# Residual scaled at its reload, score products from split halves, and half-array products side by side, in a two-layer attention and expert kernel

## The chip, the cores and the metric

The kernel runs as one program on one core of a Trainium2 chip. The metric is the device time of one execution in microseconds (us), as the median of several runs. The core's engines are named as in the profile: PE (TensorE, matrix products; PEld is its weight load), DVE (VectorE), ACT (ScalarE), POOL (GpSimd), SP (SyncE, which issues all the DMAs here).

## The reference

256 tokens of width 1024 go through two layers. Each layer is attention, a residual LayerNorm, an expert mixer (PEER) and another residual LayerNorm. Cut to what matters here:

```python
# layer 0: differential attention, 8 heads of two 64-wide maps
q, k = rope(x @ Wq), rope(x @ Wk); v = x @ Wv
s = einsum('bhmqd,bhmkd->bhmqk', q, k) * 64**-0.5        # m = 0, 1
p = softmax(where(chunk_mask, s, -inf))
o = (p[:, :, 0] - lam * p[:, :, 1]) @ v                  # RMS norm per head, then @ w_o
# layer 1: stick-breaking attention, 16 heads of 64
z = einsum('bhqd,bhkd->bhqk', q, k) * 64**-0.5
tail = reverse_cumsum(log_sigmoid(-z)) - log_sigmoid(-z)  # strictly causal
o = exp(log_sigmoid(z) + tail) @ v                       # then @ w_o
# after each sub-layer f
x = layer_norm(ALPHA * x + f(x)) * g + b
# peer(x): scores of 8 heads x 2 x 128 keys, top 16, softmax gates of 128 experts a token;
#          out = (gates * gelu(x @ u.T)) @ v, with u, v of 16384 x 1024
```

All inputs and the output are float32. The result has to agree with the float32 reference.

## The kernel before, in words

Almost all the products are of one kind. A weight row block (128x1024, 512 KB) is loaded as `raw`, ACT rounds it to `h` (L145), DVE or POOL computes the rest `l = raw - h` (L150), and PE multiplies in three passes: h by the high part of the activations (xh), l by xh, h by their low part (xl). h, l, xh and xl are float32r, a form that PE multiplies in one pass; a product of two plain float32 operands stands in the trace as two instructions that each take longer. `raw`, `h` and `l` have three buffers each. In `stationary` (L235) the weights are PE's stationary operand and the output comes transposed, in `moving_steps` (L214) the activations are.

The program in order: the Q, K and V products of layer 0 with the first attention (up to 142 us of the span), a LayerNorm, `peer` of layer 0 (routing, 128 blocks of u, then 128 blocks of v, up to 951 us), a LayerNorm, the stick-breaking attention (966 to 1097 us), a LayerNorm, `peer` of layer 1, the last LayerNorm.

**First attention.** `tr` (L396) transposes Q and K on PE, ACT copies the result to plain float32 QT and KT. `s1(i)` (L451) makes the scores of heads 2i and 2i+1 for the token blocks b=1 and b=0: for each map m and head a product with 64 rows (half of PE's 128 rows; m says which half), followed at once by a mask product over all 128 rows (L463). DVE takes the maxima (L464), ACT the exponentials (L467), DVE combines the maps (L476); `s2` transposes the result (L487), `s3` multiplies by V (L498, L500). The products of V (L440) are put between them.

**Stick-breaking attention.** `s1(h)` (L581) makes one head's scores: two products with 64 rows (L585, L586) and two mask products over 128 rows (L588, L589). ACT computes exp and ln, `s2` adds the tail by products with a triangle (L598 to L600), `s3(c)` multiplies heads 2c and 2c+1 by V, with 64 output columns each (L609, L610).

**LayerNorm.** DVE adds the residual (L273) and takes the statistics (L276), POOL the power -0.5 (L297). Token block 0 is scaled on ACT (L305), block 1 on DVE in five pieces (L324); PE transposes (L314), ACT and DVE make the next xh and xl (L330 to L332) with gain and offset applied there. The next stage's first four weight blocks were loaded ahead (`prefetch`); the first three are split in halves called `ahead`: ACT makes h, POOL l (L174), of block 0 before the LayerNorm and of blocks 1 and 2 after the second power (`hold`). After that POOL also applies gain and offset to the natural-order copy `y` (`natural`, L338, L339), which is the next residual. In `peer`, y then goes to DRAM (`xres`) and comes back near the end of `peer` for the next LayerNorm.

What sets the order: the program is written as a stream for each engine, and a scheduler with a timeline of its own places the instructions of an engine where their operands and buffers come free; inside `manual_schedule` the written order holds. The accumulator banks of tag "w" are four; scores, transposes and results of both attentions share them.

Of the kernel before, what the change touches and what calls it, by code (L numbers as in the profile page):

```python
# [10 lines left out]
F32 = mybir.dt.float32  # L11
# [9 lines left out]
P = 128  # L21
# [37 lines left out]
def trunk(ctx: ExitStack, tc: tile.TileContext, x, xT, ln_g, ln_b, w_qkv, w_o_a, lam_p, subln, w_kv,  # L59
# [60 lines left out]
    class Units:  # L120
        def __init__(self):
            self.n = 0
            self.hold = None
# [32 lines left out]
        def prefetch(self, src, raws):  # L156
            self.raws = [reg(o, D) for o in raws]
            self.pre = []
            for d, raw in enumerate(self.raws):
                self.later(raw, src(d))  # L160
            for d in range(AHEAD):
                h = [work.tile([P, 512], F32R, name="ahead", tag="hw", bufs=RING) for _ in range(2)]
                for f in range(2):
                    queue_after(nc.scalar.activation(h[f], self.raws[d][:, f * 512:(f + 1) * 512], AF.Copy), self.h)  # L164
                self.pre.append([h])
                if d == 0:
                    self.low(d)

        def low(self, d, after=None):
# [3 lines left out]
            for f in range(2):  # L173
                o = nc.gpsimd.tensor_tensor(l[f], self.raws[d][:, f * 512:(f + 1) * 512], h[f].bitcast(F32), OP.subtract)  # L174
# [6 lines left out]
        def prefetched(self):  # L181
            for d in range(1, AHEAD):
                self.low(d, self.hold)
# [73 lines left out]
    def load_gb(layer, s):  # L257
        g, bb = reg(O_G, D), reg(O_G + D, D)
# [48 lines left out]
    def layer_norm(acc, res, y, layer, s, gb, xh, xl):  # L307
# [8 lines left out]
        with tc.manual_schedule(engines={mybir.EngineType.DVE, mybir.EngineType.Activation}):  # L316
# [3 lines left out]
            units.hold = rs.second()  # L320
            mv = rs.mv[1]
            for d0, d1 in ((0, 1), (1, 2), (2, 4), (4, 6), (6, 8)):
# [13 lines left out]
        def natural():  # L336
            for b in range(NB):
                queue_after(nc.gpsimd.tensor_tensor(y[:, b, :], y[:, b, :], gb[0], OP.mult), units.hold)  # L338
                nc.gpsimd.tensor_tensor(y[:, b, :], y[:, b, :], gb[1], OP.add)  # L339

        units.natural = natural
# [35 lines left out]
    def diff_attention(xh, xl):  # L377
# [3 lines left out]
        QT, KT = reg(8192, DC, T), reg(10240, DC, T)  # L381
# [14 lines left out]
        def tr(srcv, dstT, tag):  # L396
            for b in range(NB):
                for g in range(2):
                    pt = psum.tile([P, 4, P], F32, name=tag, tag=tag)
                    for c in range(4):  # L400
                        n = 4 * g + c
                        nc.tensor.transpose(pt[:, c, :], srcv[:, b, n * P:(n + 1) * P], ident)
                    nc.scalar.activation(dstT[:, 4 * g:4 * g + 4, b * P:(b + 1) * P], pt, AF.Copy)
# [47 lines left out]
        def s1(i):  # L451
            hs = slice(2 * i, 2 * i + 2)
            for b in (1, 0):
                nk = P * (b + 1)
                p = pview(i, b)
                for m in range(2):
                    ps = psum.tile([P, 2, nk], F32, name="w", tag="w")
                    ms = slice(m * 64, (m + 1) * 64)
                    for j in range(2):
                        o = ps[:, j, :]  # L460
                        h = 2 * i + j
                        nc.tensor.matmul(o, QT[ms, h, b * P:(b + 1) * P], KT[ms, h, 0:nk], start=True, stop=False)  # L462
                        nc.tensor.matmul(o[:, nk - 64:nk], identb, bmask, start=False, stop=True)  # L463
# [83 lines left out]
        gb = load_gb(0, 0)  # L547
# [14 lines left out]
        return acc, gb  # L562


    def stick_breaking(xh, xl):
# [5 lines left out]
        units.natural()  # L571
# [9 lines left out]
        def s1(h):  # L581
            c, r = h // 2, slice((h % 2) * 64, (h % 2) * 64 + 64)
            z = psum.tile([P, 512], F32, name="w", tag="w")
            zt[h] = z
            nc.tensor.matmul(z[:, 0:256], KT[r, c, 0:P], QT[r, c, :], start=True, stop=False, skip_group_check=True)  # L585
            nc.tensor.matmul(z[:, 256:384], KT[r, c, P:T], QT[r, c, P:T], start=False, stop=False,  # L586
                             skip_group_check=True)
# [15 lines left out]
        def s3(c, oh, ol):  # L603
            o = psum.tile([P, T], F32, name="w", tag="w")
            for k in range(2):
                h, r = 2 * c + k, slice(k * 64, k * 64 + 64)
                a = ab[h]
                hs = slice(h * 64, h * 64 + 64)
                nc.tensor.matmul(o[r, :], V[:, 0, hs], a[:, 0:256], start=True, stop=False, skip_group_check=True)  # L609
                nc.tensor.matmul(o[r, P:T], V[:, 1, hs], a[:, 256:384], start=False, stop=True,  # L610
                                 skip_group_check=True)
# [3 lines left out]
        for i in range(HB + 2):  # L615
            if i < HB:
                s1(i)
            if i >= 2:
                s2(i - 2)
# [6 lines left out]
        gb = load_gb(1, 0)  # L626
# [9 lines left out]
        return acc, gb  # L636


    def peer(layer, xh, xl, spill, o_res):
# [4 lines left out]
        units.natural()  # L644
# [315 lines left out]
        for s in range(n + 1):  # L960
# [56 lines left out]
    for layer in range(2):  # L1017
        acc, gb = diff_attention(xh, xl) if layer == 0 else stick_breaking(xh, xl)
        xh, xl = xtiles()
        yv = reg(y, NB, D)  # L1020
        layer_norm(acc, reg(res, NB, D), yv, layer, 0, gb, xh, xl)
# [3 lines left out]
        if layer == 0:  # L1025
            xh, xl = xtiles()
            layer_norm(acc, reg(res, NB, D), yv, layer, 1, gb, xh, xl)
# [47 lines left out]
```

## Time and profile before

| | |
|---|---|
| runs | 1926.5 us median of 3 (1920.65 to 1926.59) |
| profiled execution | 1923.61 us, its span 1921.8 us, mean granted clock 0.982 |
| busy | PE 1853.7, DVE 1241.8, ACT 914.5, POOL 212.6 us |
| first attention, from the first score to the last | 70.1 to 109.3 us |
| three inner LayerNorms: first residual add to the dense products of the next stage | 137.6 to 153.0, 951.2 to 966.6, 1093.0 to 1108.4 us |

A busy PE is not PE at its peak: a product's end is modelled, and products that wait in a row count as busy. So the start-to-start distances in the chain of waits are what a product costs.

### The profile page before, as it was taken

To read this page: it belongs to the slowest core of one execution; us is meant where nothing else is said; L and a number is where in the kernel's file an instruction comes from. 1 tells how busy PE (TensorE), PEld (TensorE's weight loads), DVE (VectorE), ACT (ScalarE), POOL (GpSimd) and SP (SyncE) were. 2 spreads that over 40 slices of the span, in tenths; PEclk is the share of its full clock that TensorE was granted. 3 is DMA by queue.
4 is the path that set the end of the run, shared out by engine and by line. 5 is a ranking of instruction groups with operands and counts; after the bars stand their busy time and mean duration, and the time that the engine had idled before them with its cause. 6 is when DMAs were issued, how large, how long until landed. Compare 5 with 4: busy or idle time off the path is not lost.

```text
span 1921.8 us, 30897 instructions
## 1 busy us (share of the span) xinstructions
PE 1853.7 (96%) x12248; PEld 1665.9 (87%) x12248; DVE 1241.8 (65%) x2379; ACT 914.5 (48%) x1244; POOL 212.6 (11%) x208
## 2 busy tenths in 40 slices
PE   8999989999999999999999999899999999999997
PEld 7778989898899999988798699899989999999886
DVE  5467978997555555565552479789965555555655
ACT  4444444555444444454447454455544444444543
POOL 5425400000000000000142253000000000000001
PEclk9888999999999999999999999999999999999999
DMA  6433544335565555575533235443355555555653
GB/s 217 172 124 110 178 141 154 121 111 197 181 205 185 187 187 196 177 245 192 208 130 133 110 131 177 143 145 113 130 197 187 179 188 193 186 187 188 241 196 131
DMA packets 90449, 325.40 MB, mean 169 GB/s; under 512 B 10176, under 2 KB 10560, under 8 KB 89664
## 3 DMA queue, kind: packets, MB, share of 16 engines
q1 hardware_dynamic: 90304, 323.43, 49.3%
q8 instruction: 96, 1.57, 0.3%
q14 instruction: 49, 0.40, 0.1%
HBM read 320.24 MB, written 3.15 MB: 168 GB/s over the span
## 4 chain that ended last, share of the span: by engine, by line
PE 80%; DVE 16%; issue 2%; DMA 1%; ACT 1%; POOL 0%; SPq 0%; ACTq 0%; POOLq 0%
PE acc L201 40%; PE w L808 28%; PE acc L246 4%; DVE l L150 3%; DVE gl L892 2%; DVE big L865 2%; DVE gh L892 2%; PE acc L440 1%; DVE oa L896 1%; PE w L246 1%; DVE big L324 1%; PE w L201 1%; PE w L462 1%; DVE big L699 1%; DVE big L701 1%
## 5 line engine op out<-in xcount | busy, mean ns | idle before, releaser
L145 ACT ACTIVATE h<-raw 128x1024 fp32r<-128x1024 f32 x579 | 607.5, 1060 | 853.2 <-PE acc L201 474.5
L150 DVE TENSOR_TENSOR l<-raw,h 128x1024 fp32r<-128x1024 f32 x526 | 645.0, 1238 | 533.8 <-ACT h L145 533.6
L808 PE MATMUL w<-xh,l 128*128 128x256 f32 x2048 | 579.6, 284 | 16.5 <-DVE l L150 16.5
L808 PE MATMUL w<-xh,h 128*128 128x256 f32 x2048 | 585.7, 286 | 2.1 <-ACT h L145 2.1
L808 PE MATMUL w<-xl,h 128*128 128x256 f32 x2048 | 580.0, 283 | 0.0
L808 PEld LDWEIGHTS w<-xh,l 128*128 128x128 f32 x2048 | 392.5, 192 | 22.4 <-DVE l L150 17.4
L808 PEld LDWEIGHTS w<-xh,h 128*128 128x128 f32 x2048 | 393.5, 192 | 7.9 <-ACT h L145 2.5
L201 PE MATMUL acc<-h,wl 128*128 128x512 f32 x1024 | 399.1, 391 | 0.0
L201 PE MATMUL acc<-l,wh 128*128 128x512 f32 x1024 | 398.7, 390 | 0.0
L808 PEld LDWEIGHTS w<-xl,h 128*128 128x128 f32 x2048 | 393.4, 192 | 4.8
L201 PE MATMUL acc<-h,wh 128*128 128x512 f32 x1024 | 278.1, 390 | 0.0
L201 PEld LDWEIGHTS acc<-h,wl 128*128 128x128 f32 x1024 | 192.8, 188 | 36.9
L201 PEld LDWEIGHTS acc<-l,wh 128*128 128x128 f32 x1024 | 192.5, 188 | 36.4
L201 PEld LDWEIGHTS acc<-h,wh 128*128 128x128 f32 x1024 | 188.1, 188 | 35.6
L150 POOL TENSOR_TENSOR l<-raw,h 128x1024 fp32r<-128x1024 f32 x53 | 128.2, 2421 | 169.7 <-ACT h L145 156.2
L174 POOL TENSOR_TENSOR ahead<-big,ahead 128x512 fp32r<-128x512 f32 x18 | 24.0, 1361 | 752.7 <-ACT ahead L164 752.7
L951 DVE TENSOR_TENSOR wl<-big,wh 128x512 fp32r<-128x512 f32 x128 | 87.0, 687 | 6.3 <-PE acc L201 5.7
L297 POOL TENSOR_TENSOR mv<-mv,mhalf 128x1 f32<-128x1 f32 x8 | 4.9, 609 | 752.0 <-DVE mv L296 752.0
L950 ACT ACTIVATE wh<-big 128x512 fp32r<-128x512 f32 x128 | 78.2, 620 | 9.2 <-PE acc L201 4.9
L907 PE MATMUL acc<-oa,gl 128*128 128x128 f16 x512 | 66.3, 220 | 14.5 <-DVE gl L892 13.0
L906 PE MATMUL acc<-oa,gh 128*128 128x128 f16 x512 | 70.4, 220 | 0.2 <-DVE gh L892 0.2
L866 ACT ACTIVATE big<-acc 128x344 f32<-128x344 f32 x128 | 51.5, 454 | 30.7 <-DVE big L865 30.7
(215 smaller groups left out, 1841.1 us busy)
## 6 DMA issues: line engine op xcount, KB each, us to landing
raw<-in_uT SPq DMA_DIRECT2D x256, 512.0 KB, 3.3
raw<-in_v SPq DMA_DIRECT2D x256, 512.0 KB, 3.3
raw<-in_w_qkv SPq DMA_DIRECT2D x23, 512.0 KB, 4.2
raw<-in_w_kv SPq DMA_DIRECT2D x12, 512.0 KB, 4.0
raw<-in_w_o_a SPq DMA_DIRECT2D x8, 512.0 KB, 4.0
big<-in_w_pq SPq DMA_DIRECT2D x8, 512.0 KB, 6.4
raw<-in_w_pq SPq DMA_DIRECT2D x8, 512.0 KB, 5.3
raw<-in_w_q SPq DMA_DIRECT2D x8, 512.0 KB, 4.3
```

The lines of the kernel that those rows point to most:

```text
L145: self.h = nc.scalar.activation(h, raw, AF.Copy)
L150: o = e.tensor_tensor(l, raw, h.bitcast(F32), OP.subtract)
L201: nc.tensor.matmul(acc[b][f], a[:, d, ts], w[:, fs], start=(first and q == 0), stop=(last and q == 2))
L246: nc.tensor.matmul(acc[n // 2][:, n % 2, :], w[:, c:c + P], a[:, d, :], start=(d == 0 and q == 0 and n % 2 == 0), stop=(d == DC - 1 and q ...
L808: nc.tensor.matmul(ps[:, k, :], w[:, ds], a[:, d, :], start=(d == 0 and q == 0), stop=(d == DC - 1 and q == 2))
L865: nc.vector.scalar_tensor_tensor(wv[:, 0:N_STORED], pv[:, 0:N_STORED], 1.0 / GS, wv[:, 0:N_STORED], OP.mult, OP.mult)
L866: nc.scalar.activation(wv[:, N_STORED:], pv[:, N_STORED:], AF.Copy, scale=1.0 / GS)
L892: nc.vector.tensor_tensor(dst.rearrange("p r (a b) t -> p r a b t", b=16), hi[:, rs].unsqueeze(3).to_broadcast([P, 4, 8, 16, 2]), lo[:, rs ...
L906: nc.tensor.matmul(ps[:, k, :], gh[:, m, :, e], oa[:, m, :, e], start=True, stop=False)
L907: nc.tensor.matmul(ps[:, k, :], oj[:, m, :, e], oa[:, m, :, e], start=False, stop=True)
L950: nc.scalar.activation(wh, s, AF.Copy)
L951: nc.vector.tensor_tensor(wl, s, wh.bitcast(F32), OP.subtract)
```

## The change

Four edits.

1. First attention: QT and KT are each kept as two float32r tiles, high (ACT) and low (DVE, new L407); a score is three products (high by high, high by low, low by high). For each token block and head the two maps, which lie on the two halves of PE's rows, are written next to each other, in two banks. One mask product serves both heads of a map.
2. Stick-breaking: `s1(c)` takes two heads, which lie on the two halves of PE's rows, and writes their products next to each other before the masks; `s3` writes the two heads' products next to each other.
3. LayerNorm: POOL makes l of `ahead` blocks 0 and 1 before the LayerNorm, DVE that of block 2 after xl[1]; the first block's passes come as h by xh, l by xh, h by xl; DVE scales token block 1 in four pieces, not five.
4. `natural` leaves POOL. In both `peer`s y goes to DRAM unscaled; near the end gain and offset are loaded once more (to a second place) and DVE scales the reloaded residual. In the stick-breaking attention DVE scales y right behind xl[7].

```diff
+                if d < AHEAD - 1:
+                    self.low(d, nc.gpsimd)
...
         def prefetched(self):
-            for d in range(1, AHEAD):
-                self.low(d, self.hold)
+            self.low(AHEAD - 1, nc.vector, self.xhl[1][1])
...
-                seq = [(n, q) for q in range(3) for n in range(8)]
+                seq = [(n, q) for q in (0, 2, 1) for n in range(8)]
...
-            for d0, d1 in ((0, 1), (1, 2), (2, 4), (4, 6), (6, 8)):
+            for d0, d1 in ((0, 2), (2, 4), (4, 6), (6, 8)):
...
+    def natural(y, gb, after=None):
+        for b in range(NB):
+            for c, op in enumerate((OP.mult, OP.add)):
+                o = nc.vector.tensor_tensor(y[:, b, :], y[:, b, :], gb[c], op)
...
+        QT = [quad("hw", RING), quad("hw", RING)]
+        KT = [quad("hw", RING), quad("oh", OH)]
...
+                h, l = (t[i] for t in dstT)
+                nc.scalar.activation(h, pt, AF.Copy)
+                nc.vector.tensor_tensor(l, pt, h.bitcast(F32), OP.subtract)
...
-                        nc.tensor.matmul(o, QT[ms, h, b * P:(b + 1) * P], KT[ms, h, 0:nk], start=True, stop=False)
-                        nc.tensor.matmul(o[:, nk - 64:nk], identb, bmask, start=False, stop=True)
+                for j in range(2):
+                    for q, (x, y) in enumerate(((0, 0), (0, 1), (1, 0))):
+                        for m in range(2):
+                            ms = slice(m * 64, (m + 1) * 64)
+                            nc.tensor.matmul(pss[m][:, j, :], QT[x][i][ms, j, b * P:(b + 1) * P], KT[y][i][ms, j, 0:nk],
+                                             start=(j == 0 and q == 0), stop=False, skip_group_check=True)
+                for m, ps in enumerate(pss):
+                    nc.tensor.matmul(ps[:, :, nk - 64:nk], identb, bmask.unsqueeze(1).to_broadcast([P, 2, 64]),
+                                     start=False, stop=True, skip_group_check=True)
...
-        gb = load_gb(0, 0)
...
+        natural(yv, gb, units.xhl[1][DC - 1])
...
+            for z, r in zip(zs, rows):
+                nc.tensor.matmul(z[:, 0:256], KT[r, c, 0:P], QT[r, c, :], start=True, stop=False, skip_group_check=True)
+            for z, r in zip(zs, rows):
+                nc.tensor.matmul(z[:, 256:384], KT[r, c, P:T], QT[r, c, P:T], start=False, stop=False,
+                                 skip_group_check=True)
...
+            for kb, (q0, c0, c1) in enumerate(((0, 0, 256), (P, 256, 384))):
+                for k in range(2):
...
-        gb = load_gb(1, 0)
...
                 pre["gb"] = load_gb(layer, 1)
                 nc.sync.dma_start(reg(o_res, NB, D), xres)
+                natural(reg(o_res, NB, D), load_gb(layer, 0, O_G - 4096))
```

PE, first attention, scores of the first two heads for b=1, before (L462 the score, L463 its mask; w_604 and w_612 are the banks of maps 0 and 1):

```order
L462 MATMUL w_604<-big_70 128x256
L463 LDWEIGHTS identb_74
L463 MATMUL w_604<-bmask_82,identb_74 128x64
L462 MATMUL w_604<-big_70 128x256
L463 LDWEIGHTS identb_74
L463 MATMUL w_604<-bmask_82,identb_74 128x64
L462 MATMUL w_612<-big_70 128x256
```

and now (L465 the score, L468 the mask, qk the split QT and KT; w_628 and w_629 the banks of the two maps), the first six of its twelve products, and then the scores of heads 4 and 5 for b=1 (w_789, w_790):

```order
L465 MATMUL w_628<-qk_106,qk_98 128x256
L465 MATMUL w_629<-qk_106,qk_98 128x256
L465 MATMUL w_628<-qk_110,qk_98 128x256
L465 MATMUL w_629<-qk_110,qk_98 128x256
L465 MATMUL w_628<-qk_106,qk_102 128x256
L465 MATMUL w_629<-qk_106,qk_102 128x256
...
L465 MATMUL w_789<-qk_112,qk_100 128x256
L465 MATMUL w_789<-qk_108,qk_104 128x256
L468 LDWEIGHTS identb_74
L468 MATMUL w_789<-bmask_82,identb_74 128x2x64
L465 MATMUL w_790<-qk_108,qk_100 128x256
```

Of the eight blocks of twelve scores (four pairs of heads, two token blocks) two alternate between the maps as written, three have the maps one after the other without a mask between, and in three the scheduler has put one map's mask before the other map's scores.

PE, stick-breaking attention, now: the first pair of heads (L590, L592 the scores, L599, L600 the masks), and a later head, followed by an earlier head's tail products (L609 to L611):

```order
L590 MATMUL w<-big 128x256 x2
L592 MATMUL w<-big 128x128 x2
L599 LDWEIGHTS identb
...
L590 MATMUL w<-big 128x256
L592 MATMUL w<-big 128x128
...
L600 MATMUL w<-cmask,identb 128x128
L609 MATMUL w<-big,ntri 128x256
L610 MATMUL w<-big,ntri 128x128
L611 MATMUL w<-big,none_78 128x128
```

Three of the eight pairs stand next to each other as written; in five the scheduler puts one head's masks before the other's scores, as before.

DVE, near the end of layer 0's `peer`, now (L149 the weight split, L959 the split of the weighted gates, L337 the four new operations on the residual):

```order
L149 TENSOR_TENSOR l_8687<-raw_8684,h_8686 128x1024
L149 TENSOR_TENSOR l_8705<-raw_8702,h_8704 128x1024
L337 TENSOR_TENSOR big_70<-big_70 128x1024 x2
L959 TENSOR_TENSOR wl_8890<-big_70,wh_8889 128x512
L337 TENSOR_TENSOR big_70<-big_70 128x1024 x2
L149 TENSOR_TENSOR l_8736<-raw_8733,h_8735 128x1024
```

They stand in front of two weight splits; before, nothing stood there but the L959 row. On SP the four loads of gain and offset now stand together in front of the same v block's load, where two stood; their earlier places (in front of the first w_o load of each attention) are empty, and the store to `xres` has moved to before the stage's last `w_pq` load.

## Rows read from the trace of the kernel before

**Rows 1.** The profile's page: busy us of each engine, share of the span, instructions.
```profile
PE 1853.7 (96%) x12248; PEld 1665.9 (87%) x12248; DVE 1241.8 (65%) x2379; ACT 914.5 (48%) x1244; POOL 212.6 (11%) x208
```
**Rows 2.** Waits of PE: who waited for whom, us in total, times, longest.
```profile
PE w L314 <- DVE big L324: 15.0, 15, 2.4
```
**Rows 3.** Chain of waits, 60 to 180 us, by line (shares of 120 us).
```profile
by line: PE acc L246 20.1%; PE acc L440 17.4%; PE w L462 15.7%; PE acc L201 13.2%; DVE big L324 6.2%; PE w L463 3.8%; PE om L500 3.7%; issue 3.3%; PE w L487 2.7%; PE w L808 2.5%; PE om L498 2.0%; DVE l L150 1.5%; PE w L402 1.5%; DVE big L27
```
**Rows 4.** The same chain in order: start us, us, what.
```profile
54.78 5.89 PE acc L440 x26
...
86.23 6.88 PE acc L440 x18
...
109.26 2.62 PE w L487 x12
```
**Rows 5.** Stretches: us, busy us of PE, PEld, DVE, ACT, POOL (instructions), clock, DMA share, GB/s.
```profile
86.00:94.00 8.00, 8.00 (x27) 6.38 (x27) 2.42 (x8) 2.86 (x9) 2.39 (x1) 0.64 0.05 18
153.00:158.00 5.00, 5.00 (x30) 4.91 (x29) 4.75 (x5) 2.54 (x5) 4.90 (x3) 0.63 0.00 0
966.00:970.00 4.00, 4.00 (x22) 3.91 (x23) 3.72 (x6) 1.17 (x3) 3.30 (x2) 0.62 0.00 0
1022.00:1030.00 8.00, 8.00 (x43) 6.75 (x42) 2.92 (x5) 5.84 (x11) 2.42 (x1) 1.00 0.23 59
1108.00:1115.00 7.00, 7.00 (x55) 6.91 (x55) 6.69 (x9) 2.99 (x5) 4.94 (x2) 0.93 0.00 0
```
**Rows 6.** Timeline, DVE and ACT in the first attention: start, us, engine, operation.
```profile
106.92 0.47 ACT L467 ACTIVATE big<-w,big 128x256 f32<-128x256 f32 x1
...
112.31 1.41 DVE L476 SCALAR_TENSOR_TENSOR big<-big 128x128 f32<-128x128 f32 x4
```
**Rows 7.** Timeline of PE: products on half the rows, on half the columns.
```profile
1135.67 2.82 PE L665 MATMUL acc<-big 64*128 64x128 f32 x32 [1.26 <-ACT big L647]
...
1071.64 0.66 PE L609 MATMUL w<-big 128*64 128x256 f32 x4
1072.12 0.40 PE L610 MATMUL w<-big 128*64 128x128 f32 x4
1072.45 0.50 PE L201 MATMUL acc<-h,xh 128*128 128x512 f32 x1
```
**Rows 8.** Chain of waits, 984 to 1110 us, in order.
```profile
990.15 23.04 PE w L246 x192
...
1018.43 0.63 PE w L585 x2
1019.06 0.22 PE w L586 x2
...
1027.09 0.43 PE w L598 x2
```
**Rows 9.** Timeline of the first LayerNorm, DVE.
```profile
144.85 7.42 DVE L324 TENSOR_SCALAR big<-big,mv 128x128 f32<-128x128 f32 x5 [0.68 <-POOL mv L297]
...
152.76 0.42 DVE L332 TENSOR_TENSOR xl<-big,xh 128x256 fp32r<-128x256 f32 x1
...
156.24 2.04 DVE L332 TENSOR_TENSOR xl<-big,xh 128x256 fp32r<-128x256 f32 x1
```
**Rows 10.** The same stretch, POOL.
```profile
135.83 3.08 POOL L174 TENSOR_TENSOR ahead<-big,ahead 128x512 fp32r<-128x512 f32 x2 [10.15 <-ACT ahead L164]
140.65 0.55 POOL L297 TENSOR_TENSOR mv<-mv,mhalf 128x1 f32<-128x1 f32 x1 [1.74 <-DVE mv L296]
144.78 4.97 POOL L174 TENSOR_TENSOR ahead<-big,ahead 128x512 fp32r<-128x512 f32 x4
```
**Rows 11.** Near the end of layer 0's peer: ACT and DVE.
```profile
843.37 1.06 ACT L145 ACTIVATE h<-raw 128x1024 fp32r<-128x1024 f32 x1 [3.34 <-DMA raw<-in_v]
...
844.47 1.23 DVE L150 TENSOR_TENSOR l<-raw,h 128x1024 fp32r<-128x1024 f32 x1 [2.30 <-ACT h L145]
```
**Rows 12.** DMA issues: KB each, median us to landing.
```profile
big<-in_ln_b SPq DMA_DIRECT2D x4, 512.0 KB, 7.7
```

More of the change, by code (lines that the diff above doesn't have):

```diff
@@ L165, in prefetch, with low @@
                 self.pre.append([h])
-                if d == 0:
-                    self.low(d)
-        def low(self, d, after=None):
+                if d < AHEAD - 1:
+                    self.low(d, nc.gpsimd)
+        def low(self, d, eng, after=None):
             l = [work.tile([P, 512], F32R, name="ahead", tag="hw", bufs=RING) for _ in range(2)]
@@ L334, in layer_norm @@
                 units.xhl[1].append(ol)
[L336 to L341, printed above, removed]
+    def natural(y, gb, after=None):
+        for b in range(NB):
+            for c, op in enumerate((OP.mult, OP.add)):
+                o = nc.vector.tensor_tensor(y[:, b, :], y[:, b, :], gb[c], op)
+                if after:
+                    queue_after(o, after)
     def layer_norm_out(acc, res, y, gb):
@@ L380, in diff_attention, with quad @@
         TMP = reg(6144, NB, D)
-        QT, KT = reg(8192, DC, T), reg(10240, DC, T)
+        def quad(tag, bufs):
+            return [work.tile([P, 2, T], F32R, name="qk", tag=tag, bufs=bufs) for _ in range(4)]
+        QT = [quad("hw", RING), quad("hw", RING)]
+        KT = [quad("hw", RING), quad("oh", OH)]
         src = lambda c: (lambda d: W[d * P:(d + 1) * P, c * D:(c + 1) * D])
@@ L396, in tr @@
         def tr(srcv, dstT, tag):
[L397 to L403, printed above, removed]
+            for i in range(4):
+                pt = psum.tile([P, 2, T], F32, name=tag, tag=tag)
+                for j in range(2):
+                    for b in range(NB):
+                        n = 2 * i + j
+                        nc.tensor.transpose(pt[:, j, b * P:(b + 1) * P], srcv[:, b, n * P:(n + 1) * P], ident)
+                h, l = (t[i] for t in dstT)
+                nc.scalar.activation(h, pt, AF.Copy)
+                nc.vector.tensor_tensor(l, pt, h.bitcast(F32), OP.subtract)
         stats = reg(12288, 8, 2, NB, HA)
@@ L579, in stick_breaking, with s1, soft @@
         zt = {}
[L581 to L587, printed above, removed]
+        def s1(c):
+            rows = [slice(k * 64, (k + 1) * 64) for k in range(2)]
+            zs = [psum.tile([P, 512], F32, name="w", tag="w") for _ in range(2)]
+            for z, r in zip(zs, rows):
[3 more added lines that the diff above has]
+                                 skip_group_check=True)
+            for k, z in enumerate(zs):
+                zt[2 * c + k] = z
+                soft(2 * c + k, z)
+        def soft(h, z):
             nc.tensor.matmul(z[:, 0:P], identb, cmask, start=False, stop=False, skip_group_check=True)
@@ L604, in s3 @@
             o = psum.tile([P, T], F32, name="w", tag="w")
[L605 to L611, printed above, removed]
+            for kb, (q0, c0, c1) in enumerate(((0, 0, 256), (P, 256, 384))):
+                for k in range(2):
+                    h, r = 2 * c + k, slice(k * 64, k * 64 + 64)
+                    nc.tensor.matmul(o[r, q0:T], V[:, kb, h * 64:h * 64 + 64], ab[h][:, c0:c1], start=(kb == 0),
+                                     stop=(kb == 1), skip_group_check=True)
             nc.scalar.activation(oh[:, c, :], o, AF.Copy)
             nc.vector.tensor_tensor(ol[:, c, :], o, oh[:, c, :].bitcast(F32), OP.subtract)
[L615 to L619, printed above, removed]
+        for c in range(DC + 1):
+            if c < DC:
+                s1(c)
+            if c >= 1:
+                s2(2 * c - 2)
+                s2(2 * c - 1)
         av = moving(xh, xl, lambda d: w_kv[d * P:(d + 1) * P, D:2 * D], "acc")
@@ L1026, in trunk @@
             xh, xl = xtiles()
-            layer_norm(acc, reg(res, NB, D), yv, layer, 1, gb, xh, xl)
+            layer_norm(acc, reg(res, NB, D), yv, layer, 1, xh, xl)
         else:
```

31 lines of the change are left out of this document (12 added, 19 removed).

## The prediction, as recorded before the result was known

> **What bounds the kernel now.** I read the page first, then PE's waits, the chain of waits by stage, the granted clock by stage, and last the timelines of the three stages that the change touches. PE is busy for 1853.7 of 1921.8 us [rows 1], so only two things count: what PE itself has to do, and the few places where it stands still or runs slowly. The `peer` stages, three quarters of the span, are PE's own work and the change leaves their order as it is. What is left lies in the first attention, the LayerNorms and the stick-breaking attention.
>
> In the first attention the chain between 60 and 180 us runs over PE's scores for 15.7% and over their masks for 3.8% of 120 us: 18.8 + 4.6 = 23.4 us for 32 scores and 32 masks [rows 3]. Around them the granted clock falls to the lower of its two levels (1.2 GHz, 0.50 of full) for part of the time: 0.64 as a mean from 86 to 94 us [rows 5]. There 18 products of V take 6.88 us, 0.38 us each, where 26 of them before the scores take 5.89 us, 0.227 us each [rows 4]. Over the whole stage: (60 - 54.78)/0.227 = 23 of V's 96 products lie ahead of 60 us, so 73 behind it; they should take 16.5 us and take 17.4% of 120 = 20.9 us [rows 3, 4]. With 1 to 2 us on transposes and products by V (12 transposes in 2.62 us [rows 4]) that is about 6 us lost to the clock, beside what the scores themselves lose.
>
> In a LayerNorm PE waits for DVE's scaling of token block 1 (15.0 us in 15 waits, five for each of three LayerNorms [rows 2]). Its five pieces take 7.42 us [rows 9]. In the same time POOL runs four splits in 4.97 us [rows 10], 1.24 us each, and DVE's pieces come at that pace. The same shows behind it: L332 takes 2.04 us while POOL works, and 0.42 us when it does not [rows 9].
>
> **The change, part by part.**
>
> *Scores of the first attention.* A score was two instructions of a float32 product, now it is three float32r products. What such a product costs on 64 rows with both halves in turn no row shows. Below: half of the 0.120 us that a 128x256 float32r product takes (23.04 us for 192 [rows 8]), 0.06 us. Above: 0.120 us, without overlap, and 0.22 us for the 128-column ones (a float32 product of that width [rows 8]) if the narrow ones run at float32's pace. Nearest is L665, also 64 rows, one half behind the other: 32 instructions in 2.82 us, 0.088 us each [rows 7]. I take that for the five blocks without a mask between the maps: 12 x 0.088 + 2 masks x 0.14 (4.6/32) = 1.34 us, 6.7 us in all. In the three blocks with the mask between I take no overlap and 0.2 us for each of two changes between half and full rows (L585's 0.63 us against L598's 0.43 us [rows 8]): 12 x 0.120 + 0.28 + 0.4 = 2.1 us, 6.4 us in all. Together 13.1 us against 23.4: PE saves 10.3 us. If the low clock goes too, 16 us.
>
> Softmax does not shrink with PE. The last combine of maps ends at 113.7 us [rows 6], 43.6 us behind the first score. ACT's 32 exponentials at 0.47 us or less are 15 us, four combines at 1.41 us are 5.6 us [rows 6], with reductions and copies beside them. Taking 16 us out of 43.6 leaves room for either engine; PE had V's products to do meanwhile and did not wait for it. I take 12 us, nearer to the upper end, because scores now come sooner than ACT and DVE can use them and V's products fill less. The ends are 5 us (the clock stays as it is and half of the products' gain turns into waiting) and 16 us. The eight new DVE subtractions (an estimate of 0.8 us each, twice L332's 0.42 us for half the columns [rows 9]; 6.7 us) lie beside the K and V products; without that cover the first score would start 0.8 us later.
>
> *LayerNorm, three times.* POOL is now silent behind the second power, so DVE's four 128x256 pieces run alone. I take L332's 0.42 us for each, 1.7 us; the ends are 0.2 us a piece (below nothing is excluded, the work is there) and 1.5 us as now. Before, 8.2 us lie between the scaling's start at 144.85 and the dense products at 153.0 (table of the LayerNorms); six products already done in that gap are worth 0.7 us. Now: 1.7 us, 0.7 us for the last transposes, and 0.7 us more ahead of it, since POOL's first split of blocks grows from two to four operations: it starts at 135.83, two take 3.08 us, the other two about 2.5 us, so the first power can start near 141.4 instead of 140.65 [rows 10]; DVE's next step of token block 1 is queued behind the operation that waits for it. So 8.2 - 0.7 - 3.1 = 4.4 us each, 13.2 us in all. The clock gives some of it back. Today the dense products start at half clock: 0.63, 0.62 and 0.93 over 5, 4 and 7 us [rows 5] cost about 1.8, 1.5 and 0.5 us, 3.8 us in all. Starting 4.4 us sooner behind the same idle gap, I take 1.9 us each, 5.7 us. Net 13.2 + 3.8 - 5.7 = 11.3 us; ends 7 and 15 us. What was behind POOL is not missed: the split of block 2 on DVE is needed only two blocks (2 x 24 products x 0.12 = 5.8 us) later.
>
> *Stick-breaking scores.* Three pairs of heads stand side by side. Four products of these sizes on two halves of the columns take 0.81 us from the first to the next full-width product (1071.64 to 1072.45 [rows 7]); one behind the other, two heads' scores take 2 x (0.63 + 0.22) = 1.70 us [rows 8]. So 0.8 us each, 2.4 us; the last eight heads now alternate with their tail products without V's products between, so some of it goes into waiting for ACT: 2 us, ends -2 us and (all eight pairs) 6 us.
>
> *Stick-breaking `s3`.* Nothing: the two heads' products already run at the same time. Two heads' L609 together take 0.66 us, four instructions, and all four products 0.81 us [rows 7], where one behind the other would be 2 x (0.43 + 0.22) = 1.30 us. The Trainium skill (TensorE: Matmul & The Clock Gate, Part 3, on what overlaps) has matmuls start strictly in program order; by that, the first head's second product would have held back the other head's first, and writing them side by side would save 8 x 0.49 = 3.9 us. The trace does not agree: all of L609 starts before L610, though the program has L610 of the first head in between.
>
> *Residual on DVE.* In the stick-breaking attention four operations of about 1.23 us (L150's size [rows 11]) stand between the splits of weight blocks 6 and 7. PE's products cover them: seven blocks of 24 products at 0.12 us are 20 us; DVE's work ahead of block 7 is eight times two steps of about 0.5 us, four splits of 1.23 us, two of 0.7 us for block 2 and two of the four, some 17 us. Near the end of each `peer` two of the four stand before the next weight split and wait for loads that land some 7.7 us after issue [rows 12]; SP's queue holds two 512 KB loads more there, ahead of the v block for which ACT already waited 3.34 us [rows 11]. Queued behind on DVE are two weight splits, and PE waits for those. Today PE does not wait there; how much is to spare no row shows, but a block lasts 12 x 0.227 = 2.7 us and three are buffered. Two loads more and up to 5 us of DVE use most of it: I take 0.75 us for each layer, 1.5 us; ends 0 and 8 us for both. The loads that leave the attentions were hidden, and so was the store of y.
>
> Sum: 12 + 11.3 + 2 - 1.5 = 23.8 us. Against the profiled execution's own 1923.6 us this gives 1899.8 us. That execution lies 2.9 us under the median of the runs; I forecast **1901 us**, between the two ways to carry it over.
>
> **Rivals.**
>
> 1. *Softmax becomes the bound of the first attention.* For: ACT and DVE have nothing to hide behind once V's products are used up. Against: ACT's and DVE's pieces there add up to about half of the 43.6 us [rows 6]. The stage gives 4 instead of 12 us: 1909 us.
> 2. *DVE's pace in the LayerNorm is not POOL's doing.* Then four pieces at 1.5 us and the later power leave about 1 us a LayerNorm: 11.3 becomes 2 us, 1910 us. Against: the same L332 at 0.42 and 2.04 us.
> 3. *Products start in program order.* `s3` gives 3.9 us more, 1897 us. Against: all of L609 ahead of L610 [rows 7]. This is also the Trainium skill's rule cited above.
> 4. *The reload stalls PE at its upper bound,* 4 us for each layer: 1908 us.
> 5. *Slower: half-array products keep PE at the lower clock.* Place: first attention, from the first score to the last w_o product, 70 to 142 us. Those 72 us are about 53 us at full clock after the change (less 10.3 and the roughly 8 us the clock costs now). At half clock throughout they are 106 us, 34 us more than today; with the other terms 1946 us. It beats the gain from some 48 us at half clock on. For: each dip lies behind a block of 64-row scores. Against: four heads of stick-breaking scores in a row left 1.00 from 1022 to 1030 us [rows 5].
>
> **How the numbers follow.** Forecast 0.64, its own range 1891 to 1908. Rival 1: 0.11, rival 2: 0.08, rival 3: 0.05, rival 4: 0.07, rival 5: 0.03; 0.02 for no effect at all. The runs spread over 0.3%, 5.8 us, which is what can be told from no change. Range 1889 to 1913. Faster 0.93 (all but rival 5, no effect and a little of rival 2), same 0.04, slower 0.03.
>
> **What would show it.** Right: DVE's scaling pieces (now L322) near 0.4 us each; dense products of the next stage starting about 11 us behind the first residual add, not 15.4; 12 scores of a block in 1.0 to 1.5 us; last combine before 103 us; `s3` at 0.8 us for a pair, as now. Wrong: PE waiting in the first attention for ACT or DVE for more than 8 us beyond today's, clock rows of 0.6 through most of it, or a wait of PE for L149 near the two reloads of more than 2 us each.

## The result, and the profile after

The changed kernel takes 1893.4 us (median of 4 runs, 1887.7 to 1894.1) against 1924.8 us before: a ratio of 0.983, 95% interval 0.981 to 0.985. The ratios and intervals of the experiments are against the kernel before, too. The forecast was 1901 us, inside 1889 to 1913, with 0.93 on faster. The profiled execution took 1894.1 us, its span is 1892.3 us, 29.5 us less than before. Of the four executions the three with a mean granted clock of 0.989 took 1893.0 to 1894.1 us; the one with 0.992 took 1887.7, which is below the forecast's range. I cut both spans at places that both kernels have: the first residual add of each LayerNorm, and the start of the last product of the stationary block behind it. "Half clock" below is a granted clock of 0.50.

| stretch, us | before | after | gain | forecast |
|---|---|---|---|---|
| start to the first residual add of LayerNorm 1 | 137.57 | 129.03 | 8.5 | 12 |
| LayerNorm 1 with its stationary products | 39.23 | 32.20 | 7.0 | 3.8 |
| peer of layer 0 | 774.37 | 775.97 | -1.6 | -0.75 |
| LayerNorm 2 with its stationary products | 61.73 | 55.20 | 6.5 | 3.8 |
| rest of the stick-breaking attention | 80.06 | 76.97 | 3.1 | 2 |
| LayerNorm 3 with its stationary products | 37.93 | 33.09 | 4.8 | 3.8 |
| peer of layer 1 | 776.23 | 775.22 | 1.0 | -0.75 |
| last LayerNorm | 14.69 | 14.67 | 0.0 | 0 |

The page, busy us, share and instructions of each engine after the change (PE's row answers to [rows 1]):

```profile
PE 1831.4 (97%) x12264; PEld 1655.8 (87%) x12264; DVE 1232.2 (65%) x2402; ACT 911.5 (48%) x1244; POOL 176.6 (9%) x190
```

PE's waits after the change, us in total, times, longest:

```profile
PE w L312 <- DVE big L322: 3.5, 3, 1.3
PE acc L199 <- DVE l L149: 2.9, 2, 1.5
PE w L312 <- ACT big L303: 2.9, 3, 1.1
PE w L465 <- ACT big L473: 1.0, 1, 1.0
```

The 15.0 us of [rows 2] have become 3.5. The wait for ACT's scaling of token block 0 (L303) was 1.3 us before. New are two waits for a weight split (L149) and a wait of the scores for ACT (L473).

**LayerNorm.** The first LayerNorm after the change, DVE (start, us, operation; the bracket is the idle time before it):

```profile
136.59 1.39 DVE L322 TENSOR_SCALAR big<-big,mv 128x256 f32<-128x256 f32 x4 [0.68 <-POOL mv L295]
138.19 0.54 DVE L329 TENSOR_SCALAR big<-w,lnc 128x256 f32<-128x256 f32 x1 [0.22 <-ACT xh L328]
138.77 0.43 DVE L330 TENSOR_TENSOR xl<-big,xh 128x256 fp32r<-128x256 f32 x1
```

and POOL, in the same view:

```profile
127.28 5.58 POOL L173 TENSOR_TENSOR ahead<-big,ahead 128x512 fp32r<-128x512 f32 x4 [10.14 <-ACT ahead L163]
132.83 0.54 POOL L295 TENSOR_TENSOR mv<-mv,mhalf 128x1 f32<-128x1 f32 x1
135.99 0.56 POOL L295 TENSOR_TENSOR mv<-mv,mhalf 128x1 f32<-128x1 f32 x1 [2.62 <-DVE mv L294]
```

Four pieces take 1.39 us where five took 7.42 [rows 9], and POOL does nothing beside them. The dense products now start at 138.22, 9.2 us behind the first residual add; before, six of them started 12.7 us behind it and the rest at 15.4. The first power is 0.8 us late behind POOL's four splits, as priced (0.7).

The clock by stretch (us, busy us of PE, PEld, DVE, ACT, POOL, then the granted clock, DMA share, GB/s); the rows from 138 on answer to the three LayerNorm rows of [rows 5]:

```profile
71.10:129.03 57.93, 55.90 (x313) 47.28 (x313) 36.78 (x77) 34.76 (x98) 15.56 (x56) 0.85 0.36 131
138.00:143.00 5.00, 5.00 (x44) 4.97 (x43) 4.53 (x10) 3.15 (x6) 0.00 (x0) 1.00 0.51 210
946.00:950.00 4.00, 4.00 (x34) 3.88 (x34) 3.60 (x8) 2.31 (x6) 0.00 (x0) 1.00 0.00 0
1079.00:1086.00 7.00, 7.00 (x55) 7.00 (x54) 6.69 (x14) 4.92 (x9) 0.32 (x7) 0.90 0.33 136
```

Behind LayerNorms 1 and 2 the products run at full clock at once (0.63 and 0.62 before); only behind the third is a short stretch at half clock left, 3.4 us. That is one execution. In the five versions below that leave these LayerNorms as they are and were profiled once each (spread, alternate, pairs, best1, best2), four of fifteen LayerNorms have such a stretch of 3.4 us, and they are 1.2 to 1.4 us longer than the same ones without it. The kernel before has 10.3, 10.3 and 6.8 us of half clock behind its three.

**First attention.** The chain of waits after the change, in order (start, us, what); the scores are now L465:

```profile
71.17 0.91 PE w L465 x12
...
79.36 1.29 DVE big L470 x2
...
82.49 1.84 DVE big L517
...
85.08 0.81 ACT big L473 x4
...
91.44 1.75 PE w L465 x12
...
97.12 1.47 PE w L465 x6
```

Twelve scores with the maps in turn take 0.91 us (0.076 each, under the 0.088 assumed). The chain now leaves PE from 79.4 to 85.9 us: softmax on DVE and ACT ends last there. From 87.1 to 104.2 us the clock is at its half level, so later scores take longer: the six of 128 columns at 97.12 take 1.47 us, and 0.81 us in a run below (gap) where the same six come at full clock. The last combine of the maps ends at 104.9 us, later than the 103 that the prediction named as a sign.

**Reload.** DVE near the end of layer 0's peer, after:

```profile
827.26 2.36 DVE L337 TENSOR_TENSOR big<-big 128x1024 f32<-128x1024 f32 x2 [1.53 <-DMA big<-in_ln_g]
829.54 0.69 DVE L959 TENSOR_TENSOR wl<-big,wh 128x512 fp32r<-128x512 f32 x1
830.14 2.36 DVE L337 TENSOR_TENSOR big<-big 128x1024 f32<-128x1024 f32 x2
832.41 2.35 DVE L149 TENSOR_TENSOR l<-raw,h 128x1024 fp32r<-128x1024 f32 x2
```

and PE there:

```profile
833.68 0.51 PE L199 MATMUL acc<-l,wh 128*128 128x512 f32 x1 [1.38 <-DVE l L149]
```

The first pair waits for its load; the two pairs take 4.7 us, the split behind them comes late, and PE waits 1.4 us (1.5 us in layer 1).

### The profile page after: what moved, and what is told of

The parts are those of the page before. It is cut to its first block, busy times and chain, and to the rows that moved or that the text cites. A ratio compares the mean times of both kernels' runs of the same rounds, so it can differ in the third digit from the quotient of the medians.

```text
span 1892.3 us, 30931 instructions
## 1 busy us (share of the span) xinstructions
PE 1831.4 (97%) x12264; PEld 1655.8 (87%) x12264; DVE 1232.2 (65%) x2402; ACT 911.5 (48%) x1244; POOL 176.6 (9%) x190
## 4 chain that ended last, share of the span: by engine, by line
PE 77%; DVE 17%; DMA 2%; issue 2%; ACT 1%; POOL 1%; SPq 0%; POOLq 0%; ACTq 0%; DVEq 0%
PE acc L199 38%; PE w L816 28%; PE acc L244 4%; DVE l L149 3%; DVE gl L900 2%; DVE big L873 2%; DVE gh L900 2%; DVE oa L904 1%; PE w L244 1%; PE acc L444 1%; PE w L199 1%; DVE big L707 1%; DVE big L709 1%; DMA big<-in_ln_g 1%; DVE big L714 1%
## 5 line engine op out<-in xcount | busy, mean ns | idle before, releaser
L149 DVE TENSOR_TENSOR l<-raw,h 128x1024 fp32r<-128x1024 f32 x526 | 642.8, 1235 | 530.4 <-ACT h L144 530.1
L149 POOL TENSOR_TENSOR l<-raw,h 128x1024 fp32r<-128x1024 f32 x53 | 130.4, 2461 | 178.2 <-ACT h L144 167.4
L959 DVE TENSOR_TENSOR wl<-big,wh 128x512 fp32r<-128x512 f32 x128 | 87.0, 687 | 5.1 <-PE acc L199 4.7
L173 POOL TENSOR_TENSOR ahead<-big,ahead 128x512 fp32r<-128x512 f32 x12 | 16.5, 1403 | 754.2 <-ACT ahead L163 754.2
L915 PE MATMUL acc<-oa,gl 128*128 128x128 f16 x512 | 66.3, 220 | 14.2 <-DVE gl L900 12.7
```

The source lines that it names most:

```text
L149: o = e.tensor_tensor(l, raw, h.bitcast(F32), OP.subtract)
L915: nc.tensor.matmul(ps[:, k, :], oj[:, m, :, e], oa[:, m, :, e], start=False, stop=True)
L959: nc.vector.tensor_tensor(wl, s, wh.bitcast(F32), OP.subtract)
```

## The experiments

**One edit at a time.** Four kernels, each the kernel before with one of the four edits. First the scores:

```diff
+                    for q, (x, y) in enumerate(((0, 0), (0, 1), (1, 0))):
+                        for m in range(2):
...
+                            nc.tensor.matmul(pss[m][:, j, :], QT[x][i][ms, j, b * P:(b + 1) * P], KT[y][i][ms, j, 0:nk],
```

*only_scores.* 

> The kernel before with the split scores and the neighbouring maps of the first attention alone. Theory: the 8.5 us by which the changed kernel reaches the first residual add of LayerNorm 1 earlier (137.57 to 129.03 us) are all its doing, so that add stands at about 129.0 us here too and the time falls by about 8.5 us; the LayerNorms keep their slow pieces of 1.5 us and their stretches at half clock. Rival: part of it comes from the gain and offset loads that leave the queue ahead of w_o; then the add stands at 131 us or later.

Measured: ratio 0.994 (0.992 to 0.996), the first residual add at 129.38 us, every LayerNorm slow as before (39.3, 61.9 and 40.1 us). 8.2 of the 8.5 us of that stretch come with this edit alone; the half clock there is the same as in the changed kernel, from 87.1 to 104.2 us in both. The third LayerNorm, which this edit does not touch, is 2.2 us longer than before, with 10.3 us at half clock behind it, not 6.8: a difference of 1 or 2 us in one stretch of one execution can be the clock's.

Then the LayerNorm part and natural, each alone:

```diff
+            self.low(AHEAD - 1, nc.vector, self.xhl[1][1])
...
+            for d0, d1 in ((0, 2), (2, 4), (4, 6), (6, 8)):
```

```diff
+                natural(reg(o_res, NB, D), load_gb(layer, 0, O_G - 4096))
...
+        natural(yv, gb, units.xhl[1][DC - 1])
```

*only_low.* 

> The kernel before with the LayerNorm part alone (POOL splits two blocks ahead, DVE the third, four pieces, new pass order); natural stays on POOL, behind the second power. Theory 'POOL beside DVE': natural takes the place of the splits on POOL at once, so DVE's four pieces still run beside it at 1.5 us or more each and a LayerNorm gains less than 2 us; time within 5 us of before. Rival 'fewer pieces, fewer splits behind the power': the pieces fall to 0.4 us and each LayerNorm gains 4 us or more, 12 to 18 us in all.

*only_natural.* 

> The kernel before with natural alone moved to DVE; POOL still makes four splits behind the second power. Theory 'POOL beside DVE': the pieces stay at about 1.5 us while POOL splits (5 us), only what follows is faster; a LayerNorm gains 0 to 2 us, the reload costs some 3.5 us, time 1922 to 1930. Rival 'natural was what slowed DVE': pieces 0.4 us, 12 us or more faster.

Measured: 0.9964 (0.9947 to 0.9981) and 0.9971 (0.9954 to 0.9987). The three LayerNorm stretches gain 1.5, 1.1 and -0.5 us with edit 3 alone, 1.4, 1.3 and 0.8 us with edit 4 alone, 7.0, 6.5 and 4.8 us with both. So 'POOL beside DVE' holds for the sum. Some of its numbers were wrong. only_low became 0.36% faster, nearer to 7 us than to the 5 named; only_natural took 1919.3 us, under the 1922 to 1930 named, and its reload cost PE 2.1 us of waiting, not 3.5. And in only_low not every piece is slow: 8 of the 12 took 0.40 us. DVE and POOL there, the first two pieces (start, us, operation):

```profile
146.26 2.34 POOL L337 TENSOR_TENSOR big<-big 128x1024 f32<-128x1024 f32 x1
146.33 2.74 DVE L323 TENSOR_SCALAR big<-big,mv 128x256 f32<-128x256 f32 x2 [0.67 <-POOL mv L296]
```

The four pieces start at 146.33, 148.67, 148.99 and 149.32: the first ends when POOL's operation ends, the others take a third of a microsecond. Before, pieces followed each other at 1.20 to 1.29 us beside POOL operations of 1.24 us [rows 10]. A piece that starts while a POOL operation runs is held until that operation ends, however short it is itself. In only_natural it is the other way round: the four splits hold the first four pieces, 1.2 us each, and the fifth, which a POOL operation of natural held before (2.44 us), takes 0.40. So each edit alone leaves such a neighbour in place.

The heads side by side:

```diff
+            for z, r in zip(zs, rows):
+                nc.tensor.matmul(z[:, 0:256], KT[r, c, 0:P], QT[r, c, :], start=True, stop=False, skip_group_check=True)
...
+            for kb, (q0, c0, c1) in enumerate(((0, 0, 256), (P, 256, 384))):
+                for k in range(2):
```

*only_pairs.* 

> The kernel before with the two heads next to each other in the stick-breaking attention alone. Theory: the 3.1 us that this attention became shorter in the changed kernel come from the scores of the adjacent pairs, so about 3 us here, and the products by V stay at 0.8 us for a pair. Rival: they come from POOL being silent and the loads moved; then 0 to 1 us here.

Measured: 0.9974 (0.996 to 0.9987); that stretch falls from 80.06 to 76.97 us, the value of the changed kernel. The first pair, PE:

```profile
1019.15 0.70 PE L585 MATMUL w<-big 64*128 64x256 f32 x4
1019.68 0.39 PE L587 MATMUL w<-big 64*128 64x128 f32 x4
1020.00 0.23 PE L594 MATMUL w<-cmask,identb 128*128 128x128 bf16 x1
```

Two heads take 0.85 us to the first mask, which is what one head took [rows 8]. Three pairs stand like this, so the scores save 2.6 of the 3.1 us; what saves the rest no run separates.

**A longer gap without POOL.**

```diff
+            for _ in range(4):
+                nc.vector.tensor_scalar(xf[:, 0:4, :], y[:, 1, :] ..., mv[:, 0:1], mv[:, 3:4], ...)
             for d0, d1 in ((0, 2), (2, 4), (4, 6), (6, 8)):
```

*gap.* 

> The changed kernel with four more DVE operations of 128x1024 (into a scratch that is overwritten afterwards) ahead of the scaling of token block 1 in each of the three LayerNorms; POOL stays silent. They should take about 1.2 us each, so PE stands still 4.6 to 5 us longer in each. Theory: PE's standing still itself brings the half clock behind a LayerNorm; then the stretches at 0.50 come back behind all three (7 to 10 us each, 3.4 to 5 us lost each) and the time rises by 14 + about 11 = 25 us. Rival: the half clock came from something else (the single transposes between pieces held up by POOL); then no such stretch behind LayerNorms 1 and 2 and the time rises by 14 to 15 us.

Measured: 1901.7 us, 0.9888 (0.9861 to 0.9914). The LayerNorm stretches are 5.6, 5.0 and 3.6 us longer, 14.2 us in all. PE's wait for the scaling grew from 3.5 to 13.7 us, 10.2 of these 14.2. Half clock is back behind all three, 6.8 us each; the wait, and then the row of the first stretch:

```profile
PE w L312 <- DVE big L324: 13.7, 3, 4.7
```

```profile
135.00:140.00 5.00, 5.00 (x28) 5.00 (x28) 4.72 (x11) 2.99 (x5) 0.00 (x0) 0.59 0.51 210
```

So standing still alone brings half clock, as the theory said, with POOL silent. What it adds is about 4 us (14.2 - 10.2), not 11; the sum of the three stretches is the rival's number. The whole time rose by 8.3 us only, for the reason that follows.

This run showed something else. Its instructions up to the first LayerNorm are those of the changed kernel, engine by engine, yet the first add comes at 122.03 us, not 129.03. The stretch from the first score to that add in three kernels with this same order of instructions, first in gap:

```profile
70.30:122.03 51.73, 48.84 (x313) 40.53 (x313) 36.37 (x78) 34.40 (x98) 15.57 (x56) 1.00 0.42 147
```

in spread (below):

```profile
69.80:124.31 54.51, 51.62 (x313) 43.36 (x313) 36.66 (x76) 34.31 (x97) 15.58 (x56) 0.94 0.39 139
```

and in the changed kernel, the row 71.10 above: 57.93 us at 0.85. Without the time lost to the clock (1 less the granted clock, times the length) that is 51.7, 51.2 and 49.2 us; the kernel before has

```profile
70.10:137.57 67.47, 66.45 (x297) 49.28 (x297) 33.84 (x75) 35.07 (x97) 15.33 (x56) 0.85 0.34 128
```

and so 57.3 us. The edit itself is worth some 6 to 8 us at equal clock, an estimate from these four. The time lost is an upper end, since a slow clock costs nothing where PE waits for softmax: with the same instructions the stretch differs by 6.2 us, where the time lost differs by 8.5. Executions of one kernel differ too: of gap's four, three took 1901.1 to 1901.8 us at a mean granted clock of 0.989, one 1905.9 at 0.985.

**The residual's operations spread out.**

```diff
+            if late and s > len(ext) + len(fresh) + 4:
+                b, c = late.pop(0)
+                queue_after(nc.vector.tensor_tensor(r, r, gb0[c], (OP.mult, OP.add)[c]), units.o)
```

(`units.o` is the last weight split; one of the four operations in each step.)

*spread.* 

> The changed kernel with the four residual operations at the reload put behind four weight splits, one in every second block, and some three blocks later, where their loads have landed. Theory: PE's waits for a weight split there (1.4 and 1.5 us, one in each layer) come from the two operations queued in front of two splits; they vanish and the time falls by about 3 us against the changed kernel. Rival: they come from the two loads more ahead of v blocks; then they stay.

Measured: 1888.7 us, 0.9813 (0.9789 to 0.9837). Both waits are gone, and the peers take 774.3 and 774.1 us against 776.0 and 775.2: 2.8 us. All DMAs are issued in the same order in both, so the cause was the pairs in front of the splits, which waited for these loads.

**Order of half-array products forced.** The twelve scores of a block in the first attention:

```diff
+                            if last:
+                                queue_after(mm, last)
+                            last = mm
```

*alternate.* 

> The changed kernel with the twelve scores of a block of the first attention kept in the written order (maps in turn, no mask between), in all eight blocks. Theory: six products of one map in a row do not overlap (0.97 us for six of 256 columns at full clock, 1.47 to 1.58 us at half), twelve in turn take 0.91 us at full and 1.75 us at half clock; four blocks or so change, so the first residual add comes 4 to 6 us sooner. Rival: softmax sets the pace by now (PE already waited 1.0 us for an exponential, and a reduction waits for POOL); then PE waits instead and less than 1.5 us is gained.

Measured: 1888.1 us, 0.9814 (0.9789 to 0.9838); the first add at 124.43 us. Against the changed kernel's 129.03 that looks like the theory, but spread has 124.31 without this edit. Without the clock's share (54.93 us at 0.91) the stretch is 50.0 us, within the 49.2 to 51.7 of the others. So no gain of 4 to 6 us is left, and the rival fits (the scheduler moved other products of PE here too). The chain shows why:

```profile
77.97 0.44 DVE big L474
...
78.43 3.33 ACT big L477 x16
...
88.41 3.34 ACT big L477 x16
```

(L477 are the exponentials.) ACT and DVE end last where PE's scores did.

The theory's premise was also too simple. PE in gap, where all scores come at full clock (L467 the scores, L470 the masks over all rows):

```profile
88.68 1.05 PE L467 MATMUL w<-qk 64*128 64x128 f32 x12
89.66 0.28 PE L470 MATMUL w<-bmask,identb 128*128 128x128 bf16 x2
...
92.02 0.88 PE L467 MATMUL w<-qk 64*128 64x128 f32 x6
92.83 0.23 PE L470 MATMUL w<-bmask,identb 128*128 128x128 bf16 x1
92.99 0.88 PE L467 MATMUL w<-qk 64*128 64x128 f32 x6
```

Six products of one map with the mask behind them take 0.81 us. Twelve without a mask between take 0.98 us, little more. At most one of the three such blocks of this width can have the maps in turn (two of all eight blocks do, and the first, of 256 columns, is one of them), yet none takes more than 1.10 us; in turn, in alternate, they take 0.82. So what ends the overlap of the two halves is above all the full-row mask that the scheduler put between the maps.

And the four scores of two heads in the stick-breaking attention, kept in one order:

```diff
+            for i in range(3):
+                queue_after(ms[i + 1], ms[i])
```

*pairs.* 

> The changed kernel with the four scores of two heads of the stick-breaking attention kept next to each other in all eight pairs (three of eight stood so). Theory: each further pair saves what the first three saved, 3.1 us / 3, so 4 to 5 us less in this attention. Rival: ACT's three operations for a head set the pace; less than 1 us.

Measured: 1892.5 us, 0.9834 (0.981 to 0.9857); the stretch is 78.28 us, 1.3 us longer. PE's wait for ACT there, first after the change, then here:

```profile
PE w L590 <- ACT big L612: 0.3, 1, 0.3
```

```profile
PE w L590 <- ACT big L615: 1.2, 3, 0.5
```

The wait for ACT fits the rival; that it comes from a pair taking two of the four banks at once is argued, not shown. The theory had no full test: the edit keeps the order of the four scores, not their place side by side. In four of the eight pairs other products stand behind the first score (the pair then takes 0.63 + 0.85 us or more), and two of the four that stand together take 2.04 us, not 0.86.

**Versions to beat both.** best1 is spread with

```diff
-                h, l = units.get(v_src(i), "a", 2)
+                h, l = units.get(v_src(i), "a" if i < 4 else "v", 2)
...
+        wo = moving_steps(acc, oh, ol, lambda d: w_o_a[0, d * P:(d + 1) * P, :], eng="v", tail=TAIL,
```

best2 is best1 with alternate's edit; best3 is best1 with

```diff
-                if d < AHEAD - 1:
+                if d == 0:
                     self.low(d, nc.gpsimd)
...
-            self.low(AHEAD - 1, nc.vector, self.xhl[1][1])
+            for d in range(1, AHEAD):
+                self.low(d, nc.vector, self.xhl[1][d])
```

*best1.* 

> The changed kernel with the residual's operations spread as in 'spread', and the splits of V's second half and of w_o on DVE in place of DVE and POOL in turn. Theory: softmax's small operations on DVE are held up by POOL's 2.4 us splits in the first attention (one of 128x4 took 2.22 us), and softmax sets the pace there; then the stretch from the first score to the first residual add, 54.5 us with 6.8 us at half clock, becomes 2 us or more shorter and the time about 1886. Rival: DVE's eight or so splits more (1.23 us each) cost softmax as much as the holding; no change or 1 us longer.

Measured: 1885.4 us, 0.9809 (0.9788 to 0.9829). The 128x4 operation, in the changed kernel beside a POOL split from 82.14 to 84.69 us:

```profile
82.49 2.22 DVE L517 TENSOR_TENSOR big<-big 128x4 f32<-128x4 f32 x1
```

and in best1, without one:

```profile
83.61 0.16 DVE L518 TENSOR_TENSOR big<-big 128x4 f32<-128x4 f32 x1
```

The stretch is 53.31 us at clock 0.94, 1.2 us shorter than spread's at the same clock: in between, nearer to the theory. The scheduler changed PE's order here too, so the 1.2 us are not the holding's alone.

*best2.* 

> As 'best1', and the twelve scores of a block kept in the written order as in 'alternate'. Theory: with softmax setting the pace, the order of the scores is worth less than 1 us beside 'best1'. Rival: it is worth 3 us or more.

Measured: 1888.1 us, 0.9815 (0.9798 to 0.9833). No gain over best1; that fits the theory, and the clock hides a difference of a microsecond (0.88 in that stretch, 0.94 in best1).

*best3.* 

> As 'best1', and POOL splits only the first block ahead of the LayerNorm; DVE splits the second behind xl[1] and the third behind xl[2]. Theory: the first power no longer waits for two of POOL's four splits (0.8 us late in the changed kernel), so each LayerNorm with its stationary products is 0.8 us shorter, 2.4 us in all. Rival: DVE's 1.3 us more behind xl[1] make PE wait for the next xl, and nothing is gained.

Measured: 1883.5 us, 0.9793 (0.9773 to 0.9812), the lowest median of all, 10 us under the changed kernel's; its interval overlaps those of best1 and best2, so these three can't be told apart. Each of the first two LayerNorms is only 0.3 us shorter than best1's, the third is the same. The first power is on time (126.35 us, 0.1 us behind DVE); then PE waits longer for DVE's scaling (4.5 us, not 3.5) and less for ACT's (1.3, not 2.8), because the end of the last w_o products sets the second add (0.34 us of waiting on DVE). Neither number of the expectation holds.

## Why the prediction was right, and where it missed

The sum was 23.8 us, the profiled execution gained 29.5; the sign and the mechanisms were right, two sizes were not. That the whole came out as near as it did is partly luck: LayerNorm brought 7 us more than its term, the first attention 3.5 less, and the clock in that stage moves the time by as much from one execution to the next.

- *LayerNorm: 11.3 us, measured 18.4, beyond its upper end of 15.* The work was well sized: pieces of 0.35 us on average against 0.42, the late power 0.8 against 0.7. The step that failed is "Starting 4.4 us sooner behind the same idle gap, I take 1.9 us each", 5.7 us given back. The gap is not the same: it is shorter by the slow pieces (PE's wait for them fell from 15.0 to 3.5 us), and behind two of three LayerNorms the half clock is gone. 13.2 + 3.8 = 17.0 without that term; gap shows that the half clock comes back when the gap does.
- *First attention: 12 us, measured 8.5.* At full clock the eight blocks of scores and masks take 11.7 us (in gap), less than the 13.1 computed, but not as computed: products that do not overlap take 0.15 us for 256 columns, not the 0.120 taken as the upper end, and the five blocks without a mask between cost 1.0 to 1.3 us, not 1.34. In the profiled execution they take 16.0 us, because half clock stayed: 17 us of the stretch against 20 before. How much of it falls into an execution is chance as far as these runs go: with the same instructions the stage gave 8.5 us in the changed kernel, 13.3 in spread and 15.5 in gap, all inside the ends of 5 and 16. Rival 1 (softmax sets the pace) is half true: softmax does end last in parts of the stage by now, as alternate shows, but not at the price given.
- *Reload: -1.5 us.* Its waits were 2.9 us, with the mechanism as told; spread won 2.8.
- *Stick-breaking scores: 2 us, measured 3.1.* A pair saves 0.85 us (1.70 - 0.85) against the 0.8 forecast. `s3` gained nothing, as forecast: L619's eight instructions of a pair take 0.80 us to the next product. The prediction's reason is not settled, though. It compared the order of starts in the trace with the order in which the program is written, and no view shows the order that the scheduler gave to these products before the change.
- Rivals 2 to 5 did not occur.
- *Not foreseen:* peer of layer 1 gained 1.0 us in spite of its reload, because two waits at its start (1.3 us for ACT, and a part of one for DVE) fell away with a different arrival. Such a stretch varied between 773.6 and 778.4 us over all kernels run, so a term of 1 us in it can't be read from one execution.

Half clock is 69 us of the span before and 41 us after by the granted clock; each costs at most half its length, so up to 14 of the 29.5 us are the clock's. What no run settles is what makes it fall in the first attention in one execution and not in the next. Nor was the split of the scores tried without the maps side by side, so the two parts of edit 1 have no price of their own.

## What to carry to other kernels

An engine that looks slow beside another may be held by it, instruction by instruction: compare its operation's time with that of the operation running beside it, not with a share. Two edits that each leave one such neighbour in place can gain little alone and much together, so price them together. When a change shortens a standstill of PE, ask whether the half clock behind it goes as well, and compare stretches at equal clock before crediting an edit.

## What the runs showed of the hardware

A DVE multiplication, addition or subtraction on f32 data in SBUF that started while a POOL operation ran was held until that operation ended, and then took its own time. Pieces that follow each other at 0.33 us took 1.2 us beside POOL operations of 1.24 us and 2.4 us beside one of 2.34; a 128x4 operation took 2.22 us, and 0.16 us without POOL. A 128x1024 split (1.23 us alone) ended 1.08 us behind the POOL operation that it met. Not every operation was held. Those that read a PSUM bank (L331, 0.54 us) kept their time beside POOL, and so did some that read SBUF alone: the statistics (0.69 us), an addition on 128x1 (L294, 0.15 us), a reduction (L518, 0.69 us) and the searches for the largest eight in the routing (L705, 0.28 us). The Trainium skill (GPSIMD Engine Reference, Key points) says that GpSimd shares its SBUF interfaces with VectorE and that DVE instructions in a two-port mode or with two SBUF inputs contend. These runs agree for the operations with two SBUF inputs; whether the scaling pieces, which have one and were held too, ran in such a mode no view shows.

Products on the two halves of PE's rows overlapped when no full-row product stood between them: at full clock twelve of 256 columns in turn took 0.91 us, six of one half with a full-row mask behind them 0.90.
